# A two-layer attention encoder on one core: weight loads on another queue, query blocks cut another way, and four later moments in a hand-written order

## The chip, the cores and the metric

The kernel runs on one core of one Trainium2 chip. The metric is the device time of one execution in microseconds (us), as the median of several runs. A core has TensorE (PE; its weight loads are shown as PEld), VectorE (DVE), ScalarE (ACT), GpSimd (POOL) and SyncE (SP), which here only issues DMAs. All of them work through their own instructions in order and wait for each other on semaphores.

## What is computed

An encoder block of two layers on 512 tokens of width 1024, all in 32-bit floats:

```python
def reference(x, norm_gain, a_w_in, a_w_out, a_q_gain, a_k_gain, t5_bias,
              b_w_in, b_w_out, b_q_gain, b_k_gain, b_rpb):
    for i in range(DEPTH):
        hn = rms_norm(x, norm_gain[i])
        j = i // N_MIXERS
        if i % N_MIXERS == 0:
            y = mixer_a(hn, a_w_in[j], a_w_out[j], a_q_gain[j], a_k_gain[j], t5_bias)
        else:
            y = mixer_b(hn, b_w_in[j], b_w_out[j], b_q_gain[j], b_k_gain[j], b_rpb[j])
        x = x + y.astype(x.dtype)
    return x
```

Both mixers have 16 heads of 64. Layer A (`mixer_a`) has three groups of heads with dilations 1, 4 and 16: each projects queries, keys and values, norms queries and keys per head, and attends in a window; the three results are merged by their softmax denominators. Layer B (`mixer_b`) is a neighbourhood attention on a grid of 8 rows of 64 with a bias per offset. In both a gate path `silu(gate)` multiplies the result, and one output projection adds to the residual.

## The kernel before

**Products in three.** Each operand of a large product is split into a high part in the reduced 32-bit type that TensorE takes (`F32R`) and a low part, the rest. `mm3` (line 212) then issues three products: high by high, high by low, low by high. A weight tile comes as `raw`; `split` (124) casts it on ScalarE to `wh` (line 127) and subtracts on VectorE or GpSimd in a fixed pattern of three to two, to get `wl` (131). `wh` and `wl` have four buffers each, `wraw` three.

**Weights.** `blocks` and `loads` (134, 157) list all weight blocks in the order of use, cut into raw tiles of up to 1024 columns (512 KB). `raws` (166) issues a load on SyncE's queue and hands out the tile two loads later; `splits` (183) cuts each into halves, splits them, and stays three splits ahead of the products; `steps` (193) hands out what one step of products takes. A step is mostly 12 products of up to 512 columns.

**The order of the work.** Only TensorE's order is taken from the order in which the program is written down (`manual_schedule`, line 58). The other engines' instructions are ordered by a scheduler with its own estimate of times, unless an instruction is wrapped in `keep_in_program_order`, which puts it behind the one traced before it on its engine. Lines 852 to 880 interleave two generators: `main` issues the projections, `side` the attention. A clock (198, 202) adds up the estimated time of TensorE's products; `yield n` in `side` asks for a pause of n of its nanoseconds, and `yield "wait", key, n` for n after the moment at which `key` was stamped. `later_on` (226) does the same for a single DMA. So those numbers are moments in TensorE's order; nothing waits in real time because of them.

**Layer A.** It runs over eight pairs of heads (`hc`, here "pair 0" to "pair 7"). `main_a` (493) projects for each pair keys and values of groups 1 and 2 (`rawk`), the three queries with the keys of group 0 (`rawq`), then the values of group 0 (`v0_a`) and the gate (`gate_a`). `project` accumulates four blocks of 128 tokens in four PSUM tiles (`acc`); as each is done it is evacuated by ScalarE (`evac`, 422, line 444), squared on GpSimd (268) and summed on VectorE (269). `head_norm` (275) makes the scale and applies it (290). For `rawq`, `turn_q` (516) then transposes blocks of 32 by 32 in place (519). Pair 7 has its two projections in the other order, and pair 6's gate is projected after them.

**The queries' way.** What is normed has tokens on partitions; the scores want the head's 64 numbers there. After the 32 by 32 transposes the rest is a move between partitions, done through DRAM: `q_a` (521) issues four writes (532), of 32 partitions each in runs of 512 bytes, and four reads (538), one for each of group 0's keys (`k0`), and the queries of groups 0, 1 and 2 (`q0` and two parts of `q12`). All are wrapped to keep their order on SyncE's queue. `split_q` (552) makes high and low parts: `k0h` and `q0h` on ScalarE (559, 578), `k0l` and `q0l` on VectorE. The scheduler is free to place the ScalarE copies.

**Scores and weights.** `attn_a` (701) takes the four blocks of queries in two halves (`u` is 0 or 1): `scores` issues the products, `softmax` works on VectorE and ScalarE, and `turner` (670) moves the probabilities to key-major order with 32 by 32 transposes, four writes (`td<-tr`, 690) and four reads of 2 KB runs into 32 partitions each (`pt<-td`, 694). Later `weigh` (787) multiplies by the values, and `put_y` gates the result. Pairs 6 and 7 have their own moments, since no further pair follows.

**Layer B** does the same in a simpler form over eight pairs, and both layers end with `out_product` (884).

Of the kernel before, what the change touches and what calls it, by code (L numbers as in the profile page):

```python
# [13 lines left out]
F32 = mybir.dt.float32  # L14
F32R = mybir.dt.float32r
# [7 lines left out]
P = 128  # L23
S = 512
# [18 lines left out]
def tile_hybrid_encoder(  # L43
# [42 lines left out]

    ident = cp.tile([P, P], F32, name="ident")
    make_identity(nc, ident)
    ones = cp.tile([P, S], F32R, name="ones")
    nc.vector.memset(ones.bitcast(F32), 1.0)  # L90

    xm_d = dr.tile([P, KT, S], F32, name="xm_d")
# [68 lines left out]
                m = min(per, ks - k)  # L161
                yield w[:, off + k * n : off + (k + m) * n], m * n, n

    behind, begun = [], []

    def raws():
        queue = []
        for src, cols, n in loads():
            raw = wp.tile([P, 1024], F32, tag="wraw", name="wraw", bufs=3)
            dst = raw[:, :cols]  # L170
            if not begun:
                nc.sync.dma_start(dst[:, :n], src[:, :n])
                begun.append(load_x(1, 2))
                dst, src = dst[:, n:], src[:, n:]
            nc.sync.dma_start(dst, src)
            if behind:
                behind.pop()()
            queue.append((raw, cols, n))
            if len(queue) > 2:
                yield queue.pop(0)  # L180
        yield from queue

    def splits():
        queue = []
        for raw, cols, n in raws():
            step = 384 if n == 384 else 512
            for c in range(0, cols, step):
# [87 lines left out]
    def head_norm(raw, ss, ns, held):  # L275


        rs = wk.tile([P, 32], F32, tag="rs", name="rs")
        rsqrt(nc.vector if ns == 8 else nc.gpsimd, rs[:, : 4 * ns], ss[:, : 4 * ns], 4 * ns, 1.0 / DH)

        def scale():
            for i in range(4):
                by = rs[:, i * ns : (i + 1) * ns].unsqueeze(2)
                if ns == 8:
                    v = raw[:, :, i, :].rearrange("p (a b) r -> p a b r", b=2)
                    by = by.unsqueeze(3).to_broadcast([P, ns, 2, 32])
# [3 lines left out]
                m = nc.vector.tensor_mul(v, v, by)  # L290
# [127 lines left out]
    def project_qk(n, ns, key, hc, guard, first=False, **kw):  # L418
# [3 lines left out]
        def evac(i, acc):  # L422
# [97 lines left out]

    def q_a(hc):

        yield "wait", ("rawq", hc), 15000 if hc != 1 else 18000
        raw = st.pop(("rawq", hc))
        d = dr.tile([16, 32, 4, P], F32, name="qd", tag="qd", bufs=2)
        q12 = wk.tile([P, 2, 512], F32, tag="q12", name="q12", bufs=1)
        k0, q0 = (wk.tile([P, 512], F32, tag="eg", name="q0") for _ in range(2))
        lands, left = ((3, k0), (0, q0), (1, q12[:, 0, :]), (2, q12[:, 1, :])), [4]

        def write(t):  # L530
            src = raw[32 * t : 32 * t + 32].rearrange("k c i r -> k c (i r)")
            tc.keep_in_program_order(nc.sync.dma_start(d[:, :, t, :].rearrange("c k x -> k c x"), src))
            if t == 3:
                stamp["q", hc] = 0

        def read(f, dst):
            src = d[4 * f : 4 * f + 4].rearrange("a k t x -> (a k) (t x)")
            tc.keep_in_program_order(nc.sync.dma_start(dst, src))
# [12 lines left out]

    def split_q(q0, k0, q12):
# [6 lines left out]
        nc.scalar.copy(trj4(k0h), src)  # L559
        put_k([(q0h, q0l, q0)], 0)  # L560
        nc.vector.tensor_sub(trj4(k0l), src, trj4(k0h.bitcast(F32)))
        return q0h, q0l, q12, k0h, k0l

    def v_a(hc):

# [134 lines left out]

    def attn_a(hc):
        e0, e12 = st.pop(("e", hc))
        q0h, q0l, q12, k0h, k0l = st.pop(("q", hc))
        k12, v12 = st.pop(("k12", hc))
        pts, turners = [pq], []

# [2 lines left out]
        def scores(u):  # L709
# [13 lines left out]
            for t, lgs, cs, n in tiles:  # L723
                for g in range(2):
                    for j in range(4):
                        c = P * t + 32 * j
# [84 lines left out]
        if hc < NHC - 1:  # L811
            for u in range(2):
# [16 lines left out]
        else:  # L829
            for u in range(2):  # L830
# [409 lines left out]
```

## Time and profile before

| | |
|---|---|
| median of 3 runs | 868.47 us (867.72 to 869.49) |
| the profiled execution | 867.95 us, of which the span from first to last instruction is 866.1 us |
| granted TensorE clock over the span | 0.992 |
| DMA | 145.43 MB, mean 168 GB/s |
| raw weight loads | 143, of 512, 384, 256 and 192 KB |

In a timeline row stand start and length in us, engine, line, operation, output and inputs, shape and count; in brackets the engine's idle time before it and what ended it. A row of waits names who waited, for whom, the total in us, how often, and the longest. A row of stages (a:b) gives the length, then for PE, PEld, DVE, ACT and POOL the busy time with the count of instructions, then the granted TensorE clock, the share of the 16 DMA engines that was busy, and GB/s. SPq is SyncE's queue, on which DMAs are issued. In the groups by line stand the busy time in us, the mean of one in ns, and the idle time before them with what ended it.

### The profile page before, as it was taken

Reading aid. Unit: us, or ns where it says so; the run is one execution under the profiler, and the core shown is the slowest. Engines: PE = TensorE matmul, PEld = TensorE weight load, DVE = VectorE, ACT = ScalarE, POOL = GpSimd, SP = SyncE. Lnnn points to the kernel's source line nnn. Section 1 sums busy time; section 2 is a strip of 40 time slices with the busy share of each in tenths; the row PEclk is TensorE's granted clock in tenths of the full one; section 3 lists DMA queues with packets and bytes.
Section 4 is the critical chain, followed back from the end, with each engine's and each line's share of the span. In section 5 each row is a group of like instructions: output and inputs, shape, how many; then the busy total and the mean of one; then the engine's idle time right before and its main releaser. Section 6 shows DMA issues by size and latency. Waiting matters only on the chain.

```text
span 866.1 us, 15411 instructions
## 1 busy us (share of the span) xinstructions
PE 845.2 (98%) x5515; PEld 702.3 (81%) x5515; DVE 520.8 (60%) x1339; ACT 433.1 (50%) x924; POOL 304.9 (35%) x493
## 2 busy tenths in 40 slices
PE   9999998999999999999998988999999999999998
PEld 7788886788787788788787876789988999889786
DVE  7355583765674665665664855538576656766643
ACT  7434552653553553553553464436366545665541
POOL 2342432441541541541542332111444345533511
PEclk9999999899999999999999999999999999999999
DMA  6355468379478479478469196255235654556223
GB/s 246 111 158 175 147 190 232 133 204 231 139 209 241 139 193 239 137 203 231 138 173 262 49 256 183 64 180 194 80 119 155 172 169 147 153 165 182 98 91 128
DMA packets 81212, 145.43 MB, mean 168 GB/s; under 512 B 7408, under 2 KB 41136, under 8 KB 81136
## 3 DMA queue, kind: packets, MB, share of 16 engines
q1 hardware_dynamic: 80848, 144.44, 56.7%
q8 instruction: 43, 0.70, 0.4%
q14 instruction: 33, 0.27, 0.1%
q10 hardware_dynamic: 288, 0.01, 0.0%
HBM read 111.20 MB, written 33.22 MB: 167 GB/s over the span
## 4 chain that ended last, share of the span: by engine, by line
PE 76%; DMA 9%; DVE 5%; ACT 4%; POOL 3%; issue 1%; SPq 1%; ACTq 0%; DVEq 0%; POOLq 0%
PE acc L206 64%; PE log L206 4%; PE o L206 4%; DMA wraw<-in_w 3%; DMA q<-qd 3%; PE tp L210 3%; DMA qd<-rawq 1%; DMA e<-l_d 1%; POOL wl L131 1%; POOL sq L268 1%; DVE rawq L519 1%; DVE rawq L290 1%; DMA pt<-td 1%; ACT wh L127 1%; ACT rawq L444 1%
## 5 line engine op out<-in xcount | busy, mean ns | idle before, releaser
L206 PE MATMUL acc<-wh,hn_h 128*128 128x512 f32 (+1 forms) x768 | 293.3, 382 | 4.4 <-ACT rawq L444 2.4
L127 ACT CAST wh<-wraw 128x512 fp32r<-128x512 f32 (+1 forms) x276 | 161.1, 589 | 251.4 <-PE acc L206 190.8
L206 PE MATMUL acc<-wl,hn_h 128*128 128x512 f32 (+1 forms) x768 | 285.4, 372 | 0.6 <-DVE wl L131 0.6
L206 PE MATMUL acc<-wh,hn_l 128*128 128x512 f32 (+1 forms) x768 | 285.6, 372 | 0.0
L131 POOL TENSOR_TENSOR wl<-wraw,wh 128x512 fp32r<-128x512 f32 (+1 forms) x110 | 141.1, 1283 | 389.5 <-ACT wh L127 367.2
L131 DVE TENSOR_TENSOR wl<-wraw,wh 128x512 fp32r<-128x512 f32 (+1 forms) x166 | 116.8, 704 | 116.2 <-ACT wh L127 111.9
L206 PEld LDWEIGHTS acc<-wh,hn_h 128*128 128x128 f32 x768 | 144.4, 188 | 33.4 <-issue 4.0
L206 PEld LDWEIGHTS acc<-wh,hn_l 128*128 128x128 f32 x768 | 144.3, 188 | 20.6
L206 PEld LDWEIGHTS acc<-wl,hn_h 128*128 128x128 f32 x768 | 144.5, 188 | 20.0 <-DVE wl L131 0.9
L206 PE MATMUL acc<-hn_h,wh 128*128 128x512 f32 x192 | 78.6, 409 | 2.6 <-ACT rawk L444 2.3
L206 PE MATMUL acc<-hn_l,wh 128*128 128x512 f32 x192 | 75.8, 395 | 0.0
L206 PE MATMUL acc<-hn_h,wl 128*128 128x512 f32 x192 | 75.8, 395 | 0.0
L770 ACT ACTIVATE p<-p,mn 128x512 f32<-128x512 f32 (+1 forms) x64 | 45.1, 705 | 59.9 <-DVE mn L759 59.9
L609 ACT ACTIVATE p<-p,mn 128x512 f32<-128x512 f32 (+3 forms) x128 | 69.4, 593 | 2.9 <-DVE mn L608 2.9
L269 DVE TENSOR_REDUCE ss<-sq 128x4 f32<-128x256 f32 (+1 forms) x96 | 48.4, 505 | 29.2 <-POOL sq L268 28.7
L268 POOL TENSOR_TENSOR sq<-rawk 128x256 f32<-128x256 f32 x64 | 42.7, 675 | 64.9 <-ACT rawk L444 51.9
L681 DVE STREAM_TRANSPOSE tr<-p 128x512 f32<-128x512 f32 (+1 forms) x80 | 53.7, 683 | 10.4 <-ACT p L609 6.2
L206 PE MATMUL acc<-y_h,wh 128*128 128x512 f32 x128 | 52.2, 408 | 0.0
L206 PE MATMUL acc<-y_h,wl 128*128 128x512 f32 x128 | 50.0, 391 | 0.0
L206 PE MATMUL acc<-y_l,wh 128*128 128x512 f32 x128 | 50.0, 390 | 0.0
L206 PEld LDWEIGHTS acc<-hn_h,wh 128*128 128x128 f32 x192 | 36.9, 192 | 13.0 <-ACT rawk L444 4.9
L206 PEld LDWEIGHTS acc<-hn_h,wl 128*128 128x128 f32 x192 | 36.6, 191 | 8.0
(130 smaller groups left out, 1075.8 us busy)
## 6 DMA issues: line engine op xcount, KB each, us to landing
wraw<-in_w SPq DMA_DIRECT2D x95, 512.0 KB
wraw<-in_w SPq DMA_DIRECT2D x38, 384.0 KB
td<-tr SPq DMA_DIRECT2D x56, 256.0 KB
pt<-td SPq DMA_DIRECT2D x56, 256.0 KB
qd<-rawq SPq DMA_DIRECT2D x32, 256.0 KB
q<-qd SPq DMA_DIRECT2D x32, 256.0 KB
td<-tr SPq DMA_DIRECT2D x24, 224.0 KB
pt<-td SPq DMA_DIRECT2D x24, 224.0 KB
```

The lines of the kernel that those rows point to most:

```text
L127: nc.scalar.copy(h, raw)
L131: eng.tensor_sub(l, raw, h.bitcast(F32))
L206: nc.tensor.matmul(o, l, r, **kw)
L210: nc.tensor.transpose(o, i, ident)
L268: nc.gpsimd.tensor_mul(sq.rearrange("p (c r) -> p c r", r=32) if ns == 8 else sq, v, v)
L269: nc.vector.tensor_reduce(ss[:, i * ns : (i + 1) * ns], sq.rearrange("p (a b) -> p a b", b=64), axis=AX.X, op=ALU.add)
L290: m = nc.vector.tensor_mul(v, v, by)
L444: nc.scalar.activation(dst, src, AF.Copy, scale=rs_n[:, i : i + 1])
L519: nc.vector.transpose(raw[:, :, i, :], raw[:, :, i, :])
L609: nc.scalar.activation(pr, pr, AF.Copy, scale=mn[:, 3:4])
L681: nc.vector.transpose(dst, src[:, :n].rearrange("p (i b k) -> p i b k", b=4, k=32))
L770: nc.scalar.activation(row, row, AF.Exp, bias=mn[:, 1:2], scale=-1.0, accum_out=mn[:, 2:3])
```

## The change

From the fourth weight load on, ScalarE issues them, each traced right behind the first split of the tile that follows the one in use; the three at the start stay with SyncE. The queries and group 0's keys are laid out another way from the evacuation on, so that a write takes 128 partitions in runs of 2 KB and a read fills one quarter of the partitions (32) with all four kinds; one tile `qt` takes the place of `q0`, `k0` and `q12`. `k0h` is wrapped in `keep_in_program_order`. The tile of ones shrinks from 512 columns to two, and the warm-up products at the start read it with a step of 0. Some moments move: the queries' writes and reads by 500 and their splits by 1000 (pair 1: by 3000 and 2000), the second half of pair 6 by 3500, and in pair 7 one pause is 700 shorter and pair 6's products with the values come 2700 later after their stamp.

```diff
-    ones = cp.tile([P, S], F32R, name="ones")
+    ones = cp.tile([P, 2], F32R, name="ones")
...
-    behind, begun = [], []
-
-    def raws():
-        queue = []
-        for src, cols, n in loads():
+    behind, raws, todo, fetched = [], [], loads(), []
+
+    def fetch():
+
+        for src, cols, n in todo:
             raw = wp.tile([P, 1024], F32, tag="wraw", name="wraw", bufs=3)
             dst = raw[:, :cols]
-            if not begun:
+            if not fetched:
                 nc.sync.dma_start(dst[:, :n], src[:, :n])
-                begun.append(load_x(1, 2))
+                load_x(1, 2)
                 dst, src = dst[:, n:], src[:, n:]
-            nc.sync.dma_start(dst, src)
+            (nc.sync if len(fetched) < 3 else nc.scalar).dma_start(dst, src)
+            fetched.append(0)
             if behind:
                 behind.pop()()
-            queue.append((raw, cols, n))
-            if len(queue) > 2:
-                yield queue.pop(0)
-        yield from queue
+            raws.append((raw, cols, n))
+            return
 
     def splits():
         queue = []
-        for raw, cols, n in raws():
+        for _ in range(3):
+            fetch()
+        begun = False
+        while raws:
+            raw, cols, n = raws.pop(0)
             step = 384 if n == 384 else 512
             for c in range(0, cols, step):
                 queue.append((*split(raw[:, c : c + step], step), min(n, step)))
+                if c == 0 and begun:
+                    fetch()
                 if len(queue) > 3:
                     yield queue.pop(0)
+            begun = True
         yield from queue
...
-        nc.gpsimd.tensor_mul(sq.rearrange("p (c r) -> p c r", r=32) if ns == 8 else sq, v, v)
+        if ns == 8:
+            v = v.rearrange("p (a f) r -> p a f r", f=4)
+            nc.gpsimd.tensor_mul(sq.rearrange("p (f a r) -> p a f r", f=4, a=4), v, v)
+        else:
+            nc.gpsimd.tensor_mul(sq, v, v)
...
-                    v = raw[:, :, i, :].rearrange("p (a b) r -> p a b r", b=2)
-                    by = by.unsqueeze(3).to_broadcast([P, ns, 2, 32])
+                    v = raw[:, :, i, :].rearrange("p (h a f) r -> p f h a r", h=2, f=4)
+                    by = rs[:, i * ns : (i + 1) * ns].rearrange("p (f h) -> p f h", h=2)
+                    by = by.unsqueeze(3).unsqueeze(4).to_broadcast([P, 4, 2, 2, 32])
...
-        nc.tensor.matmul(busy, ones[:, :P], ones, start=True, stop=True)
+        wide = lambda n: ones[:, 0:1].to_broadcast([P, n])
+        nc.tensor.matmul(busy, wide(P), wide(S), start=True, stop=True)
...
-                pieces = [(raw[:, :, i, :], acc.rearrange("p (c r) -> p c r", r=32))]
+                src = acc.rearrange("p (f a r) -> p f a r", f=4, a=4)
+                pieces = [(raw[:, :, i, :].rearrange("p (a f) r -> p f a r", a=4), src)]
...
-        yield "wait", ("rawq", hc), 15000 if hc != 1 else 18000
+        yield "wait", ("rawq", hc), 15500 if hc != 1 else 21000
         raw = st.pop(("rawq", hc))
-        d = dr.tile([16, 32, 4, P], F32, name="qd", tag="qd", bufs=2)
-        q12 = wk.tile([P, 2, 512], F32, tag="q12", name="q12", bufs=1)
-        k0, q0 = (wk.tile([P, 512], F32, tag="eg", name="q0") for _ in range(2))
-        lands, left = ((3, k0), (0, q0), (1, q12[:, 0, :]), (2, q12[:, 1, :])), [4]
-
-        def write(t):
-            src = raw[32 * t : 32 * t + 32].rearrange("k c i r -> k c (i r)")
-            tc.keep_in_program_order(nc.sync.dma_start(d[:, :, t, :].rearrange("c k x -> k c x"), src))
-            if t == 3:
+        d = dr.tile([4, P, 512], F32, name="qd", tag="qd", bufs=2)
+        qt = wk.tile([P, 4, 4, P], F32, tag="q12", name="qt", bufs=1)
+        left = [4]
+
+        def write(a):
+            src = raw[:, 4 * a : 4 * a + 4].rearrange("p f i r -> p (f i r)")
+            tc.keep_in_program_order(nc.sync.dma_start(d[a], src))
+            if a == 3:
                 stamp["q", hc] = 0
 
-        def read(f, dst):
-            src = d[4 * f : 4 * f + 4].rearrange("a k t x -> (a k) (t x)")
+        def read(a):
+            dst = qt[32 * a : 32 * a + 32].rearrange("k t f x -> k t (f x)")
+            src = d[a].rearrange("(t k) x -> k t x", t=4)
             tc.keep_in_program_order(nc.sync.dma_start(dst, src))
             left[0] -= 1
 
-        for n in range(4):
-            later_on(700 * n, partial(write, n))
-            later_on(6800 + 700 * n, partial(read, *lands[n]))
+        for a in range(4):
+            later_on(700 * a, partial(write, a))
+            later_on(6800 + 700 * a, partial(read, a))
+
         def land():
-            yield "wait", ("rawq", hc), 27000 if hc != 1 else 30000
+            yield "wait", ("rawq", hc), 28000 if hc != 1 else 32000
             assert not left[0]
-            st["q", hc] = split_q(q0, k0, q12)
+            st["q", hc] = split_q(qt)
             yield
...
-        src = k0.rearrange("p (t j r) -> p t r j", t=4, j=4)
+        src = qt[:, :, 3, :].rearrange("p t (j r) -> p t r j", j=4)
         trj4 = lambda t: t[:, 64:EXT].rearrange("p (t r j) -> p t r j", t=4, j=4)
-        nc.scalar.copy(trj4(k0h), src)
-        put_k([(q0h, q0l, q0)], 0)
+        tc.keep_in_program_order(nc.scalar.copy(trj4(k0h), src))
+        by_t = lambda t: t.rearrange("p (t x) -> p t x", t=4)
+        put_k([(by_t(q0h), by_t(q0l), qt[:, :, 0, :])], 0)
...
-                                q12[hs, g, c : c + 32],
+                                qt[hs, t, 1 + g, 32 * j : 32 * j + 32],
...
-                    yield 11000
+                    yield 14500
...
-                yield 3200
+                yield 2500
                 if pending:
-                    yield "wait", ("gate", hc - 1), 16800
+                    yield "wait", ("gate", hc - 1), 19500
```

More of the change, by code (lines that the diff above doesn't have):

```diff
@@ L521, in q_a, with split_q @@
     def q_a(hc):
-        yield "wait", ("rawq", hc), 15000 if hc != 1 else 18000
+        yield "wait", ("rawq", hc), 15500 if hc != 1 else 21000
         raw = st.pop(("rawq", hc))
-        d = dr.tile([16, 32, 4, P], F32, name="qd", tag="qd", bufs=2)
-        q12 = wk.tile([P, 2, 512], F32, tag="q12", name="q12", bufs=1)
-        k0, q0 = (wk.tile([P, 512], F32, tag="eg", name="q0") for _ in range(2))
-        lands, left = ((3, k0), (0, q0), (1, q12[:, 0, :]), (2, q12[:, 1, :])), [4]
-        def write(t):
-            src = raw[32 * t : 32 * t + 32].rearrange("k c i r -> k c (i r)")
-            tc.keep_in_program_order(nc.sync.dma_start(d[:, :, t, :].rearrange("c k x -> k c x"), src))
-            if t == 3:
+        d = dr.tile([4, P, 512], F32, name="qd", tag="qd", bufs=2)
[5 more added lines that the diff above has]
+            if a == 3:
                 stamp["q", hc] = 0
-        def read(f, dst):
-            src = d[4 * f : 4 * f + 4].rearrange("a k t x -> (a k) (t x)")
+        def read(a):
+            dst = qt[32 * a : 32 * a + 32].rearrange("k t f x -> k t (f x)")
+            src = d[a].rearrange("(t k) x -> k t x", t=4)
             tc.keep_in_program_order(nc.sync.dma_start(dst, src))
             left[0] -= 1
-        for n in range(4):
-            later_on(700 * n, partial(write, n))
-            later_on(6800 + 700 * n, partial(read, *lands[n]))
+        for a in range(4):
+            later_on(700 * a, partial(write, a))
+            later_on(6800 + 700 * a, partial(read, a))
         def land():
-            yield "wait", ("rawq", hc), 27000 if hc != 1 else 30000
+            yield "wait", ("rawq", hc), 28000 if hc != 1 else 32000
             assert not left[0]
-            st["q", hc] = split_q(q0, k0, q12)
+            st["q", hc] = split_q(qt)
             yield
         st["land", hc] = land()
-    def split_q(q0, k0, q12):
+    def split_q(qt):
         q0h = wk.tile([P, 512], F32R, tag="q0h", name="q0h", bufs=1)
@@ L556, in split_q @@
         k0l = wk.tile([P, EXT], F32R, tag="k0l", name="k0l", bufs=1)
-        src = k0.rearrange("p (t j r) -> p t r j", t=4, j=4)
+        src = qt[:, :, 3, :].rearrange("p t (j r) -> p t r j", j=4)
         trj4 = lambda t: t[:, 64:EXT].rearrange("p (t r j) -> p t r j", t=4, j=4)
-        nc.scalar.copy(trj4(k0h), src)
-        put_k([(q0h, q0l, q0)], 0)
+        tc.keep_in_program_order(nc.scalar.copy(trj4(k0h), src))
+        by_t = lambda t: t.rearrange("p (t x) -> p t x", t=4)
+        put_k([(by_t(q0h), by_t(q0l), qt[:, :, 0, :])], 0)
         nc.vector.tensor_sub(trj4(k0l), src, trj4(k0h.bitcast(F32)))
-        return q0h, q0l, q12, k0h, k0l
+        return q0h, q0l, qt, k0h, k0l
     def v_a(hc):
@@ L702, in attn_a @@
         e0, e12 = st.pop(("e", hc))
-        q0h, q0l, q12, k0h, k0l = st.pop(("q", hc))
+        q0h, q0l, qt, k0h, k0l = st.pop(("q", hc))
         k12, v12 = st.pop(("k12", hc))
@@ L725, in scores @@
                     for j in range(4):
-                        c = P * t + 32 * j
                         for hd in range(2):
```

## The prediction

> **What bounds the kernel now.** I read the page's busy times first, then the timeline of TensorE for its idle stretches, then the timelines of the engines named as releasers, then SyncE's waits.
>
> ```profile
> span 866.1 us, 15411 instructions
> PE 845.2 (98%) x5515; PEld 702.3 (81%) x5515; DVE 520.8 (60%) x1339; ACT 433.1 (50%) x924; POOL 304.9 (35%) x493
> ...
> 151.48 0.53 PE L206 MATMUL log<-k0h,q0h 64*128 64x192 f32 x2 [4.22 <-ACT q0h L578]
> ...
> 264.82 0.50 PE L206 MATMUL acc<-wh,hn_h 128*128 128x512 f32 x1 [1.61 <-ACT gt L478]
> ...
> 475.45 0.50 PE L206 MATMUL acc<-wh,hn_h 128*128 128x512 f32 x1 [2.40 <-ACT rawq L444]
> ...
> 508.11 0.80 PE L206 MATMUL acc<-hn_h,wh 128*128 128x512 f32 x1 [2.33 <-ACT rawk L444]
> ...
> 523.83 1.46 PE L210 MATMUL tp<-ident,rawk 128*128 128x128 f32 x4 [3.09 <-DVE rawk L290]
> ...
> 665.34 1.75 PE L206 MATMUL o<-pt,rawk 128*64 128x128 f32 x24 [0.47 <-DMA pt<-td]
> ```
>
> TensorE is the bound: 98% busy, in an order fixed by the program. The change takes no product away, so all it can win is idle time. The six stalls above, the number in brackets each, sum to 14.12 us. Three of them cost more than their length, because TensorE comes back at half clock (column PEclk, behind the busy times):
>
> ```profile
> 149.40:156.20 6.80, 4.67 (x78) 3.73 (x79) 4.58 (x14) 3.44 (x8) 3.04 (x3) 0.50 0.48 168
> ...
> 507.80:511.20 3.40, 3.10 (x7) 2.51 (x8) 2.73 (x6) 2.95 (x8) 3.12 (x5) 0.50 0.60 170
> ...
> 524.90:528.30 3.40, 3.40 (x11) 2.81 (x12) 2.52 (x4) 0.00 (x0) 0.24 (x1) 0.50 0.78 229
> ```
>
> Half of the busy time there is lost: 4.67/2 = 2.33, 3.10/2 = 1.55, 3.40/2 = 1.70, together 5.58 us. So at most 14.12 + 5.58 = **19.70 us** are to be had.
>
> Behind the stalls stands one pattern, in ScalarE's timeline:
>
> ```profile
> 148.06 1.06 ACT L559 CAST k0h<-q 128x512 fp32r<-128x512 f32 x1 [6.88 <-DMA q<-qd]
> ...
> 263.14 1.14 ACT L127 CAST wh<-wraw 128x512 fp32r<-128x512 f32 x2 [6.93 <-DMA wraw<-in_w]
> ...
> 472.60 1.08 ACT L559 CAST k0h<-q 128x512 fp32r<-128x512 f32 x1 [4.32 <-DMA q<-qd]
> ...
> 474.73 2.40 ACT L444 ACTIVATE rawq<-acc,rs_n 128x512 f32<-128x512 f32 x4
> ...
> 516.07 1.14 ACT L559 CAST k0h<-q 128x512 fp32r<-128x512 f32 x1 [5.32 <-DMA q<-qd]
> ```
>
> An engine works in order: while the copy `k0h` waits for query data, the casts and the evacuations (L444) behind it wait too. At 472.60 the evacuation that TensorE needs comes after `k0h`. At 516.07 the weight casts come late, GpSimd then waits for one of them, and its norm (L119, L120) that pair 7's transposes need stands behind it:
>
> ```profile
> 518.96 1.83 POOL L131 TENSOR_TENSOR wl<-wraw,wh 128x512 fp32r<-128x512 f32 x1 [4.47 <-ACT wh L127]
> ```
>
> The data are late because SyncE issues everything, in order, and stands at weight loads that wait for a raw buffer:
>
> ```profile
> SPq L175 <- DVE wl L131: 288.7, 86, 9.8
> SPq L175 <- POOL wl L131: 72.6, 27, 5.9
> ...
> 480.20 17.23 SPq L175 DMA_DIRECT2D wraw<-in_w  x3
> 498.28 2.16 SPq L690 DMA_DIRECT2D td<-tr  x4
> 500.49 4.65 SPq L532 DMA_DIRECT2D qd<-rawq  x4
> ...
> 475.40:479.00 3.60, 3.55 (x43) 2.86 (x45) 2.04 (x5) 2.24 (x4) 3.52 (x4) 1.00 0.01 2
> ```
>
> SyncE spends 361 us waiting for DVE or GpSimd to free a raw buffer. Three weight loads spread over 17.23 us hold pair 7's query writes back to 500.49, while shortly before the DMA engines were 1% busy.
>
> **The change, part by part.**
>
> *Loads to ScalarE.* From the fourth on, about 139 of 143 loads leave SyncE's queue. Each is put behind the first cast of the next raw tile and waits there for the last split of the tile three back. Its price:
>
> ```profile
> L127 ACT CAST wh<-wraw 128x512 fp32r<-128x512 f32 (+1 forms) x276 | 161.1, 589 | 251.4 <-PE acc L206 190.8
> L131 POOL TENSOR_TENSOR wl<-wraw,wh 128x512 fp32r<-128x512 f32 (+1 forms) x110 | 141.1, 1283 | 389.5 <-ACT wh L127 367.2
> L131 DVE TENSOR_TENSOR wl<-wraw,wh 128x512 fp32r<-128x512 f32 (+1 forms) x166 | 116.8, 704 | 116.2 <-ACT wh L127 111.9
> ...
> 378.26 0.39 PE L206 MATMUL acc<-wl,hn_h 128*128 128x512 f32 x1
> ...
> 380.98 0.39 PE L206 MATMUL acc<-hn_l,wh 128*128 128x512 f32 x1
> ...
> 378.92 2.73 ACT L444 ACTIVATE rawq<-acc,rs_n 128x512 f32<-128x512 f32 x4
> ...
> 491.38 0.61 ACT L127 CAST wh<-wraw 128x512 fp32r<-128x512 f32 x1
> ...
> 493.75 0.70 DVE L131 TENSOR_TENSOR wl<-wraw,wh 128x512 fp32r<-128x512 f32 x1
> ...
> 405.65 0.36 SPq L175 DMA_DIRECT2D wraw<-in_w  x1
> ```
>
> The low half of a split (L131) takes 0.70 us on DVE or 1.28 on GpSimd after its cast; the next cast comes a step of 12 products later, 380.98 - 378.26 = 2.72 us. So as a rule the split is done when the load is reached, and ScalarE pays the issue: 139 x 0.36 = 50 us, beside 433 busy. In softmax stages it is not: after the cast of 491.38 the split of 493.75 ended 2.4 us too late. ScalarE would stand that long, with casts, exponentials and evacuations behind it, and GpSimd, DVE and at last TensorE behind those. 190.8 us of its idle time is casts waiting for TensorE, so casts run as far ahead as their buffers allow and such a delay does not show in them. It can show in an evacuation: one takes 2.73/4 = 0.68 us, and TensorE wants the first accumulator back after the last products of the other three (3 x 0.68 = 2.04), so 1.3 us are to spare. Bounds: 0, and one issue in full at two project ends of eight pairs (5.8 us). I take **1.0**, near the lower end, since 0.36 is less than 1.3. On SyncE the td, pt and query transfers no longer stand behind weights. The stall at 264.82 is a late weight load (cast at 263.14) blocking the copy of `gt`: I count its 1.61 as gone, and the 0.47 at 665.34.
>
> By the Trainium skill (DMA: Bandwidth & Descriptors, "Issuing engines are not separate DMA queues") DMAs from several engines share the same 16 engines and only the sequencer's issue time is saved. By it alone the late data would stay late; that is the second rival below. The 1% stage above shows a place where the trace speaks against it.
>
> *Blocks of 2 KB.* Writes leave from all 128 partitions in 2 KB runs, not 512 B; nearest row for their issue is td (2.16 for four) against 4.65 for four query writes. Reads now fill 32 partitions each, the form of pt<-td. Evacuation, squares and scaling walk the same elements in runs of 32; the bound above is the strided `k0h`, 1.08 against 0.59, on engines with more than 40% idle: 0. The serious point: `k0h` and `q0h` need one read each today, and all four after the change. Pair 5:
>
> ```profile
> 404.72 0.81 SPq L538 DMA_DIRECT2D q<-qd  x2
> ...
> 406.06 0.90 SPq L538 DMA_DIRECT2D q<-qd  x2
> ...
> 408.60 1.13 ACT L559 CAST k0h<-q 128x512 fp32r<-128x512 f32 x1 [4.77 <-DMA q<-qd]
> 410.26 0.73 ACT L578 ACTIVATE q0h<-q,gk 128x512 fp32r<-128x512 f32 x1 [0.52 <-DMA q<-qd]
> ...
> 411.94 0.36 PE L206 MATMUL log<-k0h,q0h 64*128 64x192 f32 x2
> ...
> 412.83 1.18 PE L206 MATMUL log<-k,q 64*32 64x128 f32 x64
> ```
>
> The first read landed 408.60 - 404.72 = 3.9 us after its issue; the last, issued at about 406.5, at the latest at 412.83, after 6.3. After the change the reads come 0.5 and the scores 1.06 us later (1000 on the planner's clock, which counts 2.56 us for the step of 2.72), so the last quarter must be there by 413.0 - 1.86 (`k0h`, `q0h`) = 411.1, that is 4.1 us after its issue. At 3.9 nothing is lost, at 6.3 it is 2.2 us a pair. Pairs 2 to 5 have this spacing: 0 to 8.8. A load (405.65) that stood ahead of the last two reads is now in another queue, so I take 0.6 a pair, **2.4**.
>
> *Pinned splits, pair 6, pair 7.* `k0h` can no longer be placed ahead of ScalarE work traced before it, so the evacuation at 474.73 goes first: 2.40 won. Pair 6's second half moves 3500 x 1.06 = 3.7 us; its softmax still overlaps the evacuation at 508.11, but the td writes of 498.28 no longer hold the transposes. Of 2.33 + 1.55 I leave **0.8** (0 to 3.9). Pair 7's query writes no longer stand behind the loads of 480.20, and its `k0h` is traced behind the transposes: of 3.09 + 1.70 I leave **0.5** (0 to 4.8).
>
> *Pair 1.* Its scores move 2.1 us, its transfer 3.2. TensorE then arrives at 147.26 + 2.1 = 149.4, and the last read must land 3.7 us after its issue. Against 3.9 that is 0.2; today's 148.06 came through engines that were full:
>
> ```profile
> 140.00:143.00 3.00, 3.00 (x15) 2.48 (x14) 0.69 (x1) 0.62 (x1) 0.00 (x0) 1.00 0.99 264
> 143.00:147.00 4.00, 4.00 (x19) 3.19 (x17) 0.00 (x0) 0.00 (x0) 0.00 (x0) 1.00 1.08 238
> ```
>
> Of 4.22 + 2.33 I leave **0.8** (0 to 6.55). The smaller `ones` shortens a memset before the warm-up products; the first real product waits for loaded data, so 0.
>
> **The sum.** 19.7 - (1.0 + 2.4 + 0.8 + 0.5 + 0.8 = 5.5) = 14.2 us. The profiled execution took 867.95 (span 866.1 and 1.8 around it), so it would take 853.7; the median of the runs shown, 868.47, lies 0.5 above it: **854.3**. With nothing left over 848.8; with the larger leftovers of two or three terms about 860.
>
> **Rivals.**
>
> *Quarters too late (slower).* `k0h` waits for the slowest of four reads, and TensorE for it, in every pair as in pair 1 today: 4 x 6.55 = 26.2 more, pair 1's 6.55 kept, the other 13.15 won: +13, **881**. It decides from 13.15/4 = 3.3 us a pair, half clock included, that is a landing some 6 to 7 us after the issue. For it: the last read may take 6.3 today, and all four are now needed. Against: loads no longer stand ahead in the same queue. The Trainium skill (SBUF — State Buffer, "Door 1: The DMA port swizzle") says that 32 partitions reach 8 of 16 ports and gives 189 against 328 GB/s, so each read would be slower by an estimate from that page of 0.6 us; no run here shows it yet. Chance 0.13.
>
> *The engines hold the transfers, not the queue.* Then pair 1 (6.55), 264.82 (1.61) and 665.34 (0.47) stay, less the 0.8 already left: 14.2 - 7.8 = 6.4 won, **862**. For it: shares of 0.99 and 1.08 above. Against: the 1% stage, and SyncE's 361 us. Chance 0.2.
>
> *The change does not do what it says:* the loads on ScalarE come as late as before, since they stand behind casts that wait for TensorE, and evacuations behind loads take what the pinning wins: **868**. Against: a cast waits only because its data are early. Chance 0.07.
>
> **How the numbers follow.** Forecast 0.6 (848.8 to 860); rivals 0.13, 0.2, 0.07. A range of 848 to 866 holds the forecast, the second rival and a little of the third: 8 in 10. Differences of 0.2% (1.7 us) can be told from none: faster 0.6 + 0.2 = 0.80, same 0.06, slower 0.13 + 0.01 = 0.14.
>
> **What would show it.** TensorE without the stalls at L578, L478, L444 and L290, and no stage at half clock after the start; SyncE's wait rows for L131 gone and a wait of some microseconds in all for loads on ScalarE. Wrong would be: new stalls `log <- ACT q0h` in pairs 2 to 5 (first rival), pair 1's stall unchanged (second), `acc <- ACT` stalls at each project's end (the 1.0 term).

## The result, and the profile after

The changed kernel takes **912.66 us** (median of 4 runs, 909.45 to 913.44); the kernel before, run beside it, 868.10 (867.12 to 869.49). The ratio is 1.0505, 95% interval 1.0476 to 1.0534: slower by 5%, where 854.3 was forecast. The profiled execution took 909.45 us.

The top of the page of after:

```profile
span 907.6 us, 15348 instructions
PE 858.7 (95%) x5515; PEld 710.9 (78%) x5515; DVE 528.4 (58%) x1339; ACT 431.4 (48%) x924; POOL 299.6 (33%) x493
```

The count of products is the same; PE fell from 98% to 95% of a longer span. The idle time between TensorE's products, added up over the groups by line, rose from 15.8 to 44.3 us. TensorE's timeline in after, rows with a wait:

```profile
59.15 0.50 PE L212 MATMUL acc<-hn_h,wh 128*128 128x512 f32 x1 [3.23 <-ACT rawq L457]
96.87 0.50 PE L212 MATMUL acc<-wh,hn_h 128*128 128x512 f32 x1 [3.33 <-ACT rawk L457]
162.91 0.79 PE L212 MATMUL acc<-wh,hn_h 128*128 128x512 f32 x1 [5.49 <-ACT rawk L457]
202.89 0.79 PE L212 MATMUL acc<-hn_h,wh 128*128 128x512 f32 x1 [4.81 <-ACT rawq L457]
276.85 0.79 PE L212 MATMUL acc<-hn_h,wh 128*128 128x512 f32 x1 [2.59 <-ACT rawq L457]
346.17 0.50 PE L212 MATMUL acc<-hn_h,wh 128*128 128x512 f32 x1 [1.96 <-ACT rawq L457]
...
512.52 0.80 PE L212 MATMUL acc<-wh,hn_h 128*128 128x512 f32 x1 [3.94 <-ACT rawq L457]
551.92 0.50 PE L212 MATMUL acc<-hn_h,wh 128*128 128x512 f32 x1 [2.62 <-ACT rawk L457]
```

The six stalls of before stood at five different things; these all stand at one, an evacuation of a projection by ScalarE (L457 is the L444 of before), and with the small ones there they are 31.1 of the 44.3 us. Behind some of them the first product runs at half clock (0.79 us in place of 0.50). The stages of after with a granted clock of 0.50:

```profile
160.25:170.49 10.24, 6.56 (x89) 4.86 (x91) 6.89 (x22) 6.79 (x15) 5.60 (x14) 0.50 0.31 100
201.21:208.04 6.83, 5.15 (x12) 4.09 (x13) 2.75 (x4) 3.50 (x7) 5.12 (x5) 0.50 1.05 234
242.17:245.58 3.41, 3.41 (x69) 2.64 (x49) 2.55 (x12) 1.64 (x5) 1.56 (x3) 0.50 0.21 85
276.30:279.72 3.42, 2.88 (x7) 2.30 (x8) 2.06 (x3) 2.73 (x5) 2.80 (x3) 0.50 1.03 259
511.82:518.65 6.83, 6.13 (x41) 5.01 (x43) 3.00 (x5) 2.89 (x6) 5.33 (x5) 0.50 0.10 27
525.48:528.89 3.41, 3.41 (x64) 2.64 (x46) 3.24 (x13) 0.00 (x0) 0.00 (x0) 0.50 0.02 5
552.78:556.20 3.42, 3.42 (x10) 2.65 (x9) 2.44 (x5) 2.98 (x8) 2.20 (x4) 0.50 0.96 208
```

Half of their 30.96 us of PE is lost: 15.5 us against 5.6 before. So 44.3 - 15.8 = 28.5 us of idle time and 9.9 us of half clock make 38.4 of the 41.5 us by which the span grew.

What holds the evacuations is in ScalarE's timeline of after. Two patterns:

```profile
57.46 0.33 ACTq L175 DMA_DIRECT2D wraw<-in_w  x1
57.89 0.62 ACT L127 CAST wh<-wraw 128x512 fp32r<-128x512 f32 x1 [6.75 <-DMA e<-l_d]
58.41 1.84 ACT L457 ACTIVATE rawq<-acc,rs_n 128x512 f32<-128x512 f32 x3
...
160.89 0.72 ACT L593 ACTIVATE q0h<-qt,gk 128x512 fp32r<-128x512 f32 x1 [8.25 <-DMA qt<-qd]
162.03 1.56 ACT L457 ACTIVATE rawk<-acc,rs_n 128x256 f32<-128x256 f32 x4
...
201.20 0.33 ACTq L175 DMA_DIRECT2D wraw<-in_w  x1
201.63 0.62 ACT L127 CAST wh<-wraw 128x512 fp32r<-128x512 f32 x1 [8.33 <-DMA pt<-td]
202.16 2.42 ACT L457 ACTIVATE rawq<-acc,rs_n 128x512 f32<-128x512 f32 x4
```

*First*, a weight load (ACTq L175) is followed at once by cast and evacuations, and the idle time before them ends, in the two rows shown, with a landing of `e` or `pt`, which are SyncE's transfers and no data of that load. The idle time is put on the cast, because issuing is not counted as work. The load at 201.20 did not wait for its buffer: the last low half that reads a raw tile before it had ended at 193.38 + 1.28 = 194.66, 6.5 us before the load went out.

```profile
193.38 1.28 POOL L131 TENSOR_TENSOR wl<-wraw,wh 128x512 fp32r<-128x512 f32 x1 [4.54 <-ACT wh L127]
```

The compiled order of after shows what such a load waits on (three neighbours on ScalarE, the first being the load of 57.46, then one row of SyncE's):

```
L175 DMACopy wraw_549<-in_w 128x1024 [waits DMAHW7_49,DVE_49,Pool_49]
L127 TensorCopy wh_545<-wraw_433 128x512 [waits DMAHW4_49,PE_49]
L457 Activation rawq_554<-acc_327,rs_n_96 128x4x4x32 [waits PE_49]
...
L664 DMACopy e12_1360<-l12_d_86 128x1x224 [waits DMAHW7_49]
```

The DMAs of SyncE and ScalarE take eight completion semaphores, DMAHW0 to DMAHW7, in turn, and a new DMA waits until the one that last used its semaphore has landed. On DMAHW7 the one before `wraw_549` is SyncE's read of `e`; the last row shows the reverse, a read by SyncE that waits for a load on ScalarE. A load on ScalarE is thereby tied to whatever was issued last on its semaphore, and holds the evacuations behind it.

The trace's records of semaphores confirm it for all six loads ahead of a rawq stall in after (issued at 57.46, 201.20, 275.16, 344.48, 411.81 and 478.88; the stall at 512.52 stands behind `q0h`): each goes out 0.10 us after a landing on its own semaphore, while VectorE and GpSimd, which free its buffer, had last reported 3.2 us or more before. Only the first two wait for a transfer of SyncE's. The other four wait for the weight load just before them on ScalarE, 7 to 8 us in flight, since writes of `td` and reads of `pt` by SyncE took the seven semaphores between:

```profile
267.97 0.34 ACTq L175 DMA_DIRECT2D wraw<-in_w  x1
...
275.16 0.33 ACTq L175 DMA_DIRECT2D wraw<-in_w  x1
```

(The profile names `pt<-td` for the idle time behind this one; by its own semaphore it is the load of 267.97.)

*Second*, `q0h` (L593) stands ahead of evacuations and of `k0h`, and waits 8.25 us for all four quarters.

### The profile page after: what moved, and what is told of

Same layout as the page of the kernel before. It is cut to its first block, busy times and chain, and to the rows that moved or that the text cites. A ratio compares the mean times of both kernels' runs of the same rounds, so it can differ in the third digit from the quotient of the medians.

```text
span 907.6 us, 15348 instructions
## 1 busy us (share of the span) xinstructions
PE 858.7 (95%) x5515; PEld 710.9 (78%) x5515; DVE 528.4 (58%) x1339; ACT 431.4 (48%) x924; POOL 299.6 (33%) x493
## 4 chain that ended last, share of the span: by engine, by line
PE 58%; DMA 17%; DVE 11%; ACT 6%; issue 3%; POOL 3%; SPq 2%; ACTq 0%; DVEq 0%; POOLq 0%
PE acc L212 46%; DMA qt<-qd 6%; PE o L212 5%; DMA qd<-rawq 4%; PE log L212 4%; DMA pt<-td 2%; DMA e<-l_d 2%; PE tp L216 2%; POOL sq L276 2%; DVE rawq L532 2%; DVE rawq L301 1%; DVE wl L131 1%; ACT wh L127 1%; SPq L544 1%; ACT p L1042 1%
## 5 line engine op out<-in xcount | busy, mean ns | idle before, releaser
L131 POOL TENSOR_TENSOR wl<-wraw,wh 128x512 fp32r<-128x512 f32 (+1 forms) x110 | 137.8, 1253 | 384.8 <-ACT wh L127 372.5
L131 DVE TENSOR_TENSOR wl<-wraw,wh 128x512 fp32r<-128x512 f32 (+1 forms) x166 | 112.9, 680 | 153.9 <-ACT wh L127 122.9
L212 PE MATMUL acc<-hn_h,wh 128*128 128x512 f32 x192 | 80.5, 419 | 18.5 <-ACT rawq L457 15.1
L276 POOL TENSOR_TENSOR sq<-rawq 128x512 f32<-128x512 f32 x32 | 34.0, 1084 | 47.2 <-ACT rawq L457 40.6
```

The lines of the kernel that those rows point to most:

```text
L131: eng.tensor_sub(l, raw, h.bitcast(F32))
L212: nc.tensor.matmul(o, l, r, **kw)
L276: nc.gpsimd.tensor_mul(sq.rearrange("p (f a r) -> p a f r", f=4, a=4), v, v)
```

## The experiments

Theories set against each other: **1**, loads on ScalarE wait for earlier transfers, SyncE's above all, through the shared semaphores (above); **2**, the four quarters land too late, with **2a**, `q0h` stands in the wrong place on ScalarE; **3**, ScalarE's time to issue is the cost. Ratios are to the kernel before, run beside each group, with 95% intervals; medians in us. The medians of before lay between 868.1 and 872.2 in these groups, so a difference between medians of two groups is known to some 4 us only.

| | kernel | median | ratio |
|---|---|---|---|
| e1 | after, loads by SyncE | 897.54 | 1.0302 (1.0248 to 1.0356) |
| e2 | after, `q0h` held | 892.35 | 1.0249 (1.0190 to 1.0308) |
| e3 | after, both | 890.65 | 1.0258 (1.0204 to 1.0312) |
| e4 | before, loads' part alone | 916.91 | 1.0530 (1.0468 to 1.0591) |
| e5 | after, loads by GpSimd | 899.49 | 1.0314 (1.0259 to 1.0370) |
| e7 | after, loads' part undone | 897.26 | 1.0285 (1.0216 to 1.0355) |
| e7p | e7, `q0h` held | 891.52 | 1.0261 (1.0209 to 1.0313) |
| e8 | before, `k0h` and `q0h` held | 864.12 | 0.9940 (0.9918 to 0.9961) |
| e9 | e8 and the layout | 899.91 | 1.0337 (1.0277 to 1.0397) |
| e10 | e8 and the moments | 861.57 | 0.9925 (0.9902 to 0.9948) |
| e11 | e8, pair 1's split later | 860.61 | 0.9912 (0.9883 to 0.9940) |
| e12 | e3, the split 5000 later | 870.95 | 1.0013 (0.9990 to 1.0036) |
| f1 | e12, loads by ScalarE | 910.85 | 1.0461 (1.0408 to 1.0515) |
| f2 | e12, loads by GpSimd | 865.49 | 0.9939 (0.9913 to 0.9965) |
| f3 | e8, queries' moments, pair 1 at 34000 | 859.85 | 0.9880 (0.9828 to 0.9931) |
| f5 | f3, loads by GpSimd | 862.09 | 0.9929 (0.9903 to 0.9955) |

### The loads: e4, e1, e5

e4 is the kernel before with `fetch` and `splits` of the change and nothing else.

> The kernel before with the loads' part of the change alone (issued by ScalarE, called inside the splits); layout, order and moments as before. Theory 1: rawq and rawk evacuations wait behind a load as in the changed kernel, some 10 to 20 us of new gaps and half clock: 880 to 895 us. Theory 3, issue time only, as the prediction had it: 868 to 874 us. Theory 2, the blocks are the whole cause: 862 to 869 us.

Measured 916.91: this part alone is slower than the whole change. ScalarE's timeline and TensorE's waits in e4:

```profile
265.92 0.33 ACTq L175 DMA_DIRECT2D wraw<-in_w  x1
266.35 0.62 ACT L127 CAST wh<-wraw 128x512 fp32r<-128x512 f32 x1 [7.58 <-DMA e<-l_d]
266.87 2.42 ACT L450 ACTIVATE rawq<-acc,rs_n 128x512 f32<-128x512 f32 x4
```

```profile
PE acc L212 <- ACT rawq L450: 23.7, 7, 5.0
PE acc L212 <- ACT rawk L450: 8.2, 8, 3.0
```

The first pattern, without the layout and without the moments: 31.9 us of TensorE's idle time at evacuations, against 4.7 in before. Theory 1's number was too low, its place right; theory 3's 868 to 874 fails.

```diff
-            (nc.sync if len(fetched) < 3 else nc.scalar).dma_start(dst, src)
+            nc.sync.dma_start(dst, src)
```

> The changed kernel with all weight loads issued by SyncE, the loads still called where the change calls them. Theory 1 (a weight load in ScalarE's order waits until SyncE's earlier transfer on the same completion semaphore has landed, and holds the evacuations behind it): the gaps before the rawq evacuations at 55.92, 198.09, 274.26, 344.21, 412.46 and 479.10 us (3.2 + 4.8 + 2.6 + 2.0 + 1.1 + 1.5 = 15.2 us) go, with 5 to 10 us of the half clock behind them: 887 to 898 us. The gaps behind q0h (93.53, 157.42, 508.58) stay. Theory 2 (the four quarters land later and everything waits for them): the same reads are there, the gaps stay, 905 us or more. Theory 3 (the 139 issues of 0.36 us on ScalarE are the cost): also faster, but the weight splits and not the evacuations ahead of a project's end get shorter waits.

897.54, at the edge of theory 1: all six rawq gaps are gone. What was not expected are gaps in front of the scores of pairs 2 to 6 (1.9, 5.6, 3.8, 2.7 and 2.6 us), of which those of pairs 3 to 6 are new or longer.

e5 has `nc.gpsimd` in the place of `nc.scalar`.

> The changed kernel with the weight loads issued by GpSimd in place of ScalarE. It tells whether the wait is for SyncE's transfers through shared completion semaphores, or comes with any second engine. Theory 1: if GpSimd's transfers have completion semaphores of their own, ScalarE is free and the rawq gaps (15.2 us) go as with SyncE: 887 to 900 us, less if GpSimd's own issue time delays the low halves that it makes. If a load waits for the transfers of any queue, GpSimd's low halves wait in their turn and the stalls come back as waits for wl: 905 us or more.

899.49, within theory 1's range: all six rawq gaps are gone. The one behind `q0h` in pair 7 stays (5.5 us), and the transposes of `rawk`, whose norm is made on GpSimd, wait 6.7. In e5's compiled order GpSimd's loads take other semaphores, DMASW0 to DMASW7, so that they are tied only to each other:

```
L175 DMACopy wraw_352<-in_w 128x1024 [waits DMASW2_49,DVE_49]
```

### `q0h`'s place: e2, e3, e7, e7p, e8

`put_k` passes the instruction through `keep_in_program_order` where `split_q` calls it:

```diff
-            nc.scalar.activation(dh, src, AF.Copy, scale=gk[:, g : g + 1])
+            held(nc.scalar.activation(dh, src, AF.Copy, scale=gk[:, g : g + 1]))
```

> The changed kernel with q0h held in program order behind k0h. Theory 2a (q0h, which waits for all four quarter reads, was put ahead of evacuations and splits on ScalarE): the gaps at 93.53 (3.3), 157.42 (5.5), 238.06 and 240.22 (2.7), 508.58 (3.9) and the six k0l gaps (about 4) go or shrink to under a fifth, with 5 us of half clock: 890 to 900 us; the rawq gaps stay at about 15 us. Theory 1 alone: the time stays within 5 us of 912, since ScalarE's loads still wait. Should q0h's wait only come at another place (late quarters), the gaps move to products of the scores and the time stays over 905 us.

892.35, 20.3 us faster than after: theory 2a holds for pairs 0, 2 and 6, though the gaps did not shrink to a fifth (at 93 us 3.3 became 0.8, at 238 to 240 us 2.7 became 1.3, at 508 us 3.9 became 1.3); pair 1's stayed (5.2). The rawq gaps stayed, as it said.

> The changed kernel with both repairs: weight loads issued by SyncE (as e1, 897.5 us) and q0h held behind k0h (as e2, 892.4 us). If the two causes add (Theory 1: the loads, 15.1 us; Theory 2a: q0h ahead of evacuations, 20.3 us): 875 to 880 us. e1 also shows new gaps in front of the scores (5.6, 3.8, 2.7, 2.6, 1.9 us), which name the quarter reads as late when SyncE's loads stand ahead of them: if these stay, the time is 880 to 890 us. Below 866 only if the change's other parts gain what the prediction gave them (about 18 us).

890.65, no better than e2 beyond the intervals: the two repairs don't add. TensorE's waits say why, e2 first, then e3:

```profile
PE acc L212 <- ACT rawq L457: 12.9, 6, 4.1
PE log L212 <- ACT q0h L593: 8.1, 4, 5.2
```

```profile
PE log L212 <- ACT q0h L593: 17.2, 6, 5.3
```

With the loads back on SyncE 12.9 us at evacuations went, and 9.1 us came in front of the scores: there the loads stand ahead of the quarter reads.

> The changed kernel with the loads' part undone in full: issued by SyncE and called where the kernel before calls them, three ahead. Layout, held k0h and later moments stay. Against e1 it tells the place of the call from the engine. If the place does nothing: 893 to 902 us, as e1. If the loads' earlier place is better for the splits or puts the quarters earlier on SyncE: 870 to 890 us. The prediction's rival of late quarters, by itself: 881 us.

897.26, as e1: the place of the call does nothing that shows.

> The kernel of e7 with q0h held behind k0h: only layout, held splits and moments are changed against the kernel before. If the loads and q0h's place are the whole of the loss, this shows what the prediction promised without them: 850 to 866 us. If the four quarters land too late for the scores' moments: 868 to 885 us, with gaps in front of the scores that name k0h and the reads.

891.52, above the 868 to 885 given for late quarters: layout, holds and moments by themselves lose 2.6%. So the loads are not the whole cause; theory 2 stands beside theory 1.

> The kernel before with k0h and q0h held in program order and nothing else changed. If the gaps at 475 and 508 us and pair 1's come from k0h standing ahead of evacuations on ScalarE (the prediction's step for the pin): 3 to 7 us faster, 861 to 866 us. If they come from transfers that land late: within 2 us of 868.

864.12: holding both is worth 0.6%. The stalls of before at 475 and 524 us are gone, that at 508 us is 1.0; 2.2 us in front of pair 6's scores are new, and pair 1's gap is 6.0.

### The quarters and the moments: e9, e10, e11, e12

> The kernel before with the layout part (2 KB runs, four quarters) and k0h and q0h held in order; loads and moments as before. Set against e8 (864.1 us, the same holds without the layout). The packets of a quarter read take 156 ns where the reads of before took 84, and k0h needs the last of four reads where it needed the first. Theory 2 (late quarters): gaps of 2 to 5 us in front of the scores of pairs 2 to 5 as in e3 and e7p (1.7, 1.8, 1.9, 5.2 and 2.1, 5.5, 2.2, 1.6 us), 880 to 892 us. If those gaps came from the later moments and not from the layout: 862 to 868 us. The prediction's size for the quarters, 0.6 us a pair: 866 to 867 us.

899.91, slower by more than theory 2 gave. TensorE's waits in e9:

```profile
PE log L206 <- ACT q0h L587: 25.5, 6, 8.0
```

SyncE's timeline in its pair 2:

```profile
217.41 0.49 SPq L175 DMA_DIRECT2D wraw<-in_w  x1
218.01 1.08 SPq L545 DMA_DIRECT2D qt<-qd  x2
222.44 0.35 SPq L175 DMA_DIRECT2D wraw<-in_w  x1
222.85 0.90 SPq L545 DMA_DIRECT2D qt<-qd  x2
```

ScalarE's at the same place:

```profile
230.61 1.07 ACT L567 CAST k0h<-qt 128x512 fp32r<-128x512 f32 x1 [4.17 <-DMA qt<-qd]
```

and TensorE's:

```profile
232.35 0.35 PE L206 MATMUL log<-k0h,q0h 64*128 64x192 f32 x2 [3.18 <-ACT q0h L587]
```

Two reads go out at 218, a load then holds SyncE until 222.44, and the last read follows at about 223.4; `k0h` starts 7.2 us after it. With the old layout the first of the four would have been enough, issued 5.4 us earlier. The trace's DMA records add that the 2 KB packets after the first reads take 168 and 174 ns (medians of 222 to 223 and 223 to 224 us), against 84 in e8 (216 to 218 us); the first 94 of the 250 that moved from 221 to 224.5 us took 84 here too. Of the 25.5 us, 8.0 are pair 1's, which stalls for 6.0 us in e8 with the old layout.

> The kernel before with k0h and q0h held in order and the five moments of the change; layout and loads as before. Against e8 (864.1 us). The prediction gave pair 1's moment 0.8 us and pair 6's 0.8 us of gain on top of the holds: 860 to 863 us. If the gap of pair 1 (6.0 us in e8) stays and pair 6's second half only turns a gap at 509 us into one on its softmax (e3: 1.7 + 1.2 us): 864 to 868 us.

861.57, 2.6 us below e8, with intervals that overlap: when the layout and the loads are away, the moments at least don't harm. Pair 1's gap fell from 6.0 to 1.1 us; pair 7's transposes wait 1.7 and 1.16 us more.

> e8 with one number changed: the moment at which pair 1's q is split and its scores follow, 30000 to 36000 cycles of the plan; its transfer stays where it is. e8 has one large gap left, 6.0 us at 149.36 us, where k0h waits 5.8 us for pair 1's read. If that read is simply late against its moment: the gap goes with its half clock, 855 to 859 us, faster than both kernels. If the later scores push the same wait into the next pair: 862 to 866 us.

```diff
-            yield "wait", ("rawq", hc), 27000 if hc != 1 else 30000
+            yield "wait", ("rawq", hc), 27000 if hc != 1 else 36000
```

860.61, between the two ranges: the gap of 6.0 us went, and 4.0 us came in front of the weighing, which now waits for pair 1's softmax.

> e3 (loads by SyncE, q0h held) with the moment of the split 5000 later (28000 to 33000, pair 1 32000 to 37000); the transfers stay. Theory 2 says that what is left in e3 is the wait for the last quarter; with 5 us more the gaps in front of the scores (5.3, 1.7, 1.8, 1.9, 5.2, 1.3 us) go to under 1 us each: 865 to 876 us. If they are not the quarters' lateness, or come back as waits of the weighing for the later softmax: 885 to 895 us.

```diff
-            yield "wait", ("rawq", hc), 28000 if hc != 1 else 32000
+            yield "wait", ("rawq", hc), 33000 if hc != 1 else 37000
```

870.95 against 890.65: 5 us more before the split takes away 19.7, so lateness was most of the price of the layout. Not all of the 19.7 is the layout's: pair 1's 5.3 us of waiting in e3, now 0.5, has its like in the old layout (6.0 in e8), where a later split takes it away too (e11). What is left is 5.7 us in pair 7 and some gaps of 0.5 to 1.9.

### Both causes apart: f1, f2, f3, f5

f1 and f2 differ from e12 only in the engine that issues the loads from the fourth on: `nc.scalar` and `nc.gpsimd`.

> e12 (870.95 us: q0h held, the split of q 5000 later) with the loads issued by ScalarE again. Theory 1, loads on ScalarE wait for SyncE's transfers by themselves: the rawq gaps come back (2.2, 4.1, 3.4, 0.9, 0.4, 1.9 us in e2, 12.9 in all) with some half clock: 884 to 895 us. If the loads on ScalarE cost only through the late quarters: 868 to 874 us.

910.85: with everything else equal, ScalarE costs 39.9 us against SyncE. ScalarE's waits in f1:

```profile
ACT wh L127 <- DMA pt<-td: 44.2, 6, 9.2
...
ACT wh L127 <- DMA e<-l_d: 12.4, 4, 6.0
```

and TensorE's:

```profile
PE acc L212 <- ACT rawq L457: 27.1, 6, 6.3
```

f1 waits twice as long at rawq as e2 did (27.1 against 12.9): with the scores moved, other transfers fall in front of the loads. By the semaphores all six loads wait for SyncE's here (`e`, `td` and four times `pt`), where in e2 four waited for the load before. The price of this tie depends on what happens to be in flight, and my 12.9 for it was too low.

> The same with the loads issued by GpSimd. If the wait belongs to the completion semaphores that SyncE's and ScalarE's transfers share: no rawq gaps, 865 to 876 us, as e12 or a little better, since SyncE is rid of the loads. If any second engine pays for it: 884 to 895 us as f1.

865.49, 5.5 us faster than e12. TensorE's two longest waits in f2; there is no row for rawq at all:

```profile
PE log L212 <- ACT q0h L593: 6.4, 2, 5.8
PE o L212 <- DVE mn L773: 3.6, 5, 0.7
```

> The kernel before with k0h and q0h held, the transfer at 15500 and 21000 and the split at 28000, pair 1 34000; no layout, no loads, nothing of pair 6's and 7's other moments. e10 had 2.9 us of gaps in front of tp (1.7 and 1.16 us) and 1.9 us at pair 1; both should go: 854 to 859 us, faster than both kernels and than e10 and e11. If pair 1's wait only moves on to the weighing (4.0 us in e11): 859 to 862 us.

859.85, ratio 0.9880: faster than both kernels, with nothing but the two holds and the queries' moments (15500 and 21000; 28000 and 34000). It is just outside the hoped 854 to 859; 2.4 us at the evacuation of `rawk` at 503 us and 1.5 us for `pt` are new. By the medians it is 1.7 us ahead of e10 and 0.8 of e11, less than the intervals can tell.

> f3 (859.85 us) with the weight loads issued by GpSimd inside the splits. f3 has few gaps left that a load or SyncE's queue could be the cause of (2.4 us of rawk at 502.84, 1.5 us of pt at 532.29). If SyncE rid of the loads brings the blocks and the weights' transposes earlier and GpSimd's issues cost nothing: 854 to 858 us. If GpSimd's issues delay its low halves and the scale of q: 860 to 868 us.

862.09: on the old layout GpSimd's loads bring nothing.

## Why the prediction was wrong

**The bound and the 19.70 us to be had: right as far as the runs tell.** The moments and holds, the parts that went for that idle time, win together where the loads and the layout are away (e10, f3); the most that was had is 1.2%, some 10 us.

**The term of 1.0 for the loads: the step that failed first.** It said that "ScalarE pays the issue" and that the only wait is for the split. SyncE's waits for L131 are gone as forecast, but the loads took another wait with them, for the landing of the DMA that last used their semaphore, with ScalarE idle for up to 8.3 us at a time in after and 9.2 in f1. The upper bound, 5.8, was an issue in full at each project's end; measured are 15.1 us of rawq stalls in after (without the 3.9 at 512.52, which stand behind `q0h`), 27.1 in f1, 39.9 us of time in f1 against e12. The trace of before had the sign of it, in SyncE's waits:

```profile
SPq L175 <- DMA e<-l_d: 8.4, 5, 2.3
SPq L690 <- DMA wraw<-in_w: 4.5, 5, 1.4
```

A weight load (L175) waited there for the landing of `e`, and a td write (L690) for a weight load, neither of which it needs. I took the load to wait for the split only. No run separates ScalarE's 50 us of issue time, which theory 3 would charge, from the wait; but GpSimd spends 80 us on the same 139 issues in f2 (0.576 us each) and nothing is lost by it.

**The term of 2.4 for the quarters: wrong in size, by both of its inputs.** It took the last read to land 3.9 to 6.3 us after its issue; `k0h` started 7.2 us after it in e9, and the last two reads were issued 3.8 us late, behind a load (219.1 to 222.85). The clause "a load that stood ahead of the last two reads is now in another queue" held for the changed kernel: in e2, where the loads are on ScalarE, pairs 2 to 5 lose 2.9 us in front of the scores (1.31, 1.12, 0.45 and nothing over 0.1), near the 2.4. But there TensorE also stood 12.9 us at evacuations, which gives the reads time. In e5, with hardly such stalls, it is 8.7 (1.11, 3.25, 2.93 and 1.46), the upper bound. So the rival *quarters too late* was the right mechanism for a good part: e7p, which has it alone, took 891.52 against its 881. Its condition, "a landing some 6 to 7 us after the issue", was met.

The Trainium skill (SBUF — State Buffer, "Door 1: The DMA port swizzle") was cited for 0.6 us more per read. This case's trace agrees in part: 128 packets of 2 KB on 16 engines at 84 and at 168 ns are 0.67 and 1.34 us, 0.67 more, but in e9 only some 156 of the 250 packets were that slow, so an estimate from them is 0.4 us a read. It was the smaller part of the lateness.

**Held splits: right for `k0h`, and half a step.** I followed `k0h` behind the evacuation of 474.73 and did not ask where the scheduler would put `q0h`, which nothing holds and which now waits for four reads too. It went ahead of `k0h` and of evacuations: 20.3 us between after and e2. With both held the step is right (e8, 0.6% faster).

**Pair 1, pairs 6 and 7: right mechanisms, covered by the rest.** In after pair 1's stall is 5.49 us, now at `rawk`. In e10, without layout and loads, 1.09 and three gaps of 0.1 to 0.5 are left of it, against the 0.8 given. Pair 6's second half and pair 7's transposes keep 1.36, 1.70 and 1.16 us in e10, more than the 0.8 and 0.5 that were left for them; f3, which leaves those moments as they were, does no worse.

**The rival *engines hold the transfers, not the queue*: half right.** By the Trainium skill (DMA: Bandwidth & Descriptors, "Issuing engines are not separate DMA queues") another issuing engine saves issue time alone. The old layout agrees: GpSimd's loads gain nothing in f5. In the new layout they gain 5.5 us (f2 against e12), and the gaps of 1.5 and 1.8 us at `q0h` in pairs 2 and 4 of e12 are gone: SyncE no longer holds quarter reads behind a load. So the issuing order, and not the DMA engines alone, made reads late there.

**The rival *the change does not do what it says*: near, for another reason.** It had evacuations wait behind loads, as they do, but only while casts wait for TensorE, and for no more than the pinning wins (868). The loads waited at their semaphores, and e4, which has them alone, took 916.91.

**Left open.** No run has loads on ScalarE with semaphores of their own. That the shared semaphores and not ScalarE as such are the wait is read from the compiled order, from the landing 0.10 us before each of these loads (all six ahead of a rawq stall in after, e2 and f1 alike), and from GpSimd's loads, which have others. A fourth raw buffer was not tried. Why the loads in flight took 7 to 8 us is not separated either; the DMA engines were 83 to 89% busy meanwhile.

## What to carry to other kernels

Before moving a DMA to an engine that computes, list every wait that the DMA has, its completion semaphore too, and what stands behind it there; an in-order engine whose evacuations TensorE needs was the worst of the three places tried here. When a transfer is cut another way, count how many pieces the first consumer needs, and move its moment by the landing of the last one. When one instruction is held in order, hold all that wait for the same data.

## What the runs showed of the hardware

A gap does not always bring the half clock. In after 2.59 us at 274 us was followed by 0.50, and so was the pair of 0.68 and 1.08 at 522 to 524; the gaps of 3.23 and 3.33 at 59 and 97 us were not (products of 0.50 us at once). So a gap's length alone did not tell whether its products would run at half clock. The evacuation of the queries costs the same in both layouts (689 ns before, 686 after) and their scaling less in the new one (824 and 721 ns): runs of 32 elements in another order cost nothing that shows there. A DMA that waited for a landing on its own semaphore went out 0.10 us after it.
